# The order of the twelve matrix products of a weight load in the input projection of a hybrid block

## The chip, the cores and the metric

The kernel runs on one core of one Trainium2 chip. The metric is the device time of one execution in microseconds (us): the median of three runs for the kernel before. One further execution was profiled; its span and its trace are what is read here. Engines are named as in the profile: PE is TensorE's matmul, PEld its weight load, DVE is VectorE, ACT is ScalarE, POOL is GpSimd, SP is SyncE, which issues most DMAs.

## What is computed

One layer of a backbone block on 256 latent tokens, with 256 context tokens in front of them, all in float32 and width 2048. Both token sets are normalised and modulated, and multiplied with the input projection `w_in`; its columns feed four groups of mixers: gated linear attention (GLA), gated DeltaNet (GDN), a short convolution, and RWKV-7. The recurrent ones scan forwards and backwards; they run on the context first, and their final states start the latent scans. Then come the output projection `w_out`, a gated residual, a SwiGLU feed-forward part and a final norm.

```python
def _mix(n, row_len, init, lp):
    (g_q, ..., r_wa, r_g) = jnp.split((n @ lp['w_in']).astype(jnp.float32), offs, axis=-1)
    ...                                   # GLA, GDN, short convolution, RWKV-7 on these columns
    y = jnp.concatenate([y_gla, y_gdn, y_sc, y_rw], axis=-1)
    return y @ lp['w_out'], states

o_c, ctx_states = _mix(modnorm(ctx), len_ctx, zero, lp)
o_x, _ = _mix(modnorm(x), GRID_W, ctx_states, lp)
h_x = h_x + m_x[2] * o_x
h_x = h_x + m_x[5] * swiglu(modnorm(h_x), w_gu, w_down)
return rmsnorm(h_x, final_g)
```

## The kernel before

**Precision.** A float32 product is made of three faster ones. Each operand is split in an upper part, rounded to the matmul's short format (`wh`, `H`), and the rest (`wl`, `L`): `wh H + wh L + wl H`. ACT makes `wh` from the raw weights (L197), then DVE subtracts to get `wl` (L202). Matmuls of the recurrent mixers are not split; PE runs each of them as two pieces (a transpose as one), and the profile counts pieces.

**The projection.** `proj` makes one tile of 128 output columns by 256 tokens in PSUM (`big`, two buffers). It goes over the 16 slices of the width in four loads (`hf`). A load takes 512 columns of weights by DMA into `wraw` (a ring of six), splits them into `wh` and `wl` (rings of three), and then makes 4 slices x 3 = 12 products; the accumulation starts with the first product of the tile and ends with the last. There are 66 tiles, so 264 loads and 3168 products. Between load and products up to two pieces of other work are taken from `feed`: matmuls `ob`, which make the later modulation vectors during the context stage.

**The mixers.** Two streams of recurrent work run side by side: stream a (RWKV-7; tiles `ea`, `la`, `iva...`, `rw_...`) and stream b (GDN and GLA; `eb`, `lb`, `ivb...`, `gd_...`). Each is a chain of small matmuls with steps on ACT, DVE or POOL between them. A GLA pair does for each direction: scores (`eb<-gd_q,gd_Fb`), transposes (`eb<-ident,gd_Fg`), and four scan steps of matmuls into `lb`, with the state `gd_S` between them; after both directions a sum for the norm (`lb<-gd_tok,ones`), and then the result goes as `yH`, `yL` to the output projection.

**What sets the order.** The table `ORDER` lists the parts (RWKV, GDN, GLA, projections to be parked in DRAM, short convolutions), with an offset of priority for some. Tile's scheduler then orders each engine's instructions when the program is built: of what is ready in its own account of time, it issues what has the highest priority. Loads and splits of weights stand in `high_priority`, so they run as early as their rings allow; products have their part's priority. Each engine works through its order strictly, and waits where an input is missing. The output projection (`wout`, L1486 on) uses the same rings; for the first two column blocks it goes over the tiles 12 to 15, 4 to 11 and then 0 to 3, which GLA makes; each load gives six products on 512 columns.

Of the kernel before, what the change touches and what calls it, by code (L numbers as in the profile page):

```python
# [18 lines left out]
KT = D // P  # L19
# [156 lines left out]
def block_kernel(ctx: ExitStack, tc: tile.TileContext, x, cx, ada_first, ada_later, ada_b, w_in, w_early, w_out,  # L176
# [11 lines left out]
    def mk(pool, shape, tag, bufs=None, dt=F32):  # L188
        pool = sub.get(tag[:3], pool) if pool is sub.get("mx") else pool
        return pool.tile(list(shape), dt, tag=tag, name=nm(tag), bufs=bufs)  # L190
# [22 lines left out]
    def mm(o, l, r, start=True, stop=True):  # L213
        return TE.matmul(o, l, r, start=start, stop=stop)  # L214
# [35 lines left out]
    def wraw():  # L250
        return mk(wp[0], [P, wp[1]], "wraw", wp[3])

    def split(raw, who, pool=None):

        n = 2 if pool else wp[2]
        h = mk(pool or wp[0], [P, wp[1]], "wh", n, F32R)
        l = mk(pool or wp[0], [P, wp[1]], "wl", n, F32R)

        n = 2 if wp[1] == 1024 else 1
        w = wp[1] // n  # L260
        for i in range(n):
            sl = slice(i * w, (i + 1) * w)
            acopy(h[:, sl], raw[:, sl])
            tt(l[:, sl], raw[:, sl], h.bitcast(F32)[:, sl], SUB, e=who)
        return h, l
# [120 lines left out]
    with ExitStack() as st:  # L386
# [76 lines left out]
        for kt in range(KT):  # L463
# [4 lines left out]
            with tc.issue_after(ins if kt != KT - 2 else after):  # L468
                for i in range(NE):
                    o = acc[i // 2][:, i % 2]  # L470
                    a, b = wh[:, i * P:(i + 1) * P], wl[:, i * P:(i + 1) * P]
# [40 lines left out]
    with mix:  # L512
# [36 lines left out]
        def PB(shape, tag="e"):  # L549

            tag = tag if tag == "big" else tag + cur[0]
            return mk(pb, shape, tag, 2 if tag in ("big", "ea") else 1)
# [43 lines left out]
        def proj(nHL, which):  # L596

            r0 = TIDX[which] * P
            H, L = nHL
            ps = PB([P, T], "big")  # L600
            for hf in range(4):
                with tc.high_priority():
                    raw = wraw()
                    nc.sync.dma_start(raw, w_in[r0:r0 + P, hf * 512:(hf + 1) * 512])
                    wh, wl = split(raw, V)
                for f in feed[:2]:
                    f()
                del feed[:2]
                for k in range(4):
                    kt = hf * 4 + k  # L610
                    a, b = wh[:, k * P:(k + 1) * P], wl[:, k * P:(k + 1) * P]
                    mm(ps, a, H[kt], kt == 0, False)
                    mm(ps, a, L[kt], False, False)
                    mm(ps, b, H[kt], False, kt == KT - 1)
            return ps

        def pcol(nHL, name, i):
            return proj(nHL, (name, i))
# [813 lines left out]
        for tok in ORDER:  # L1432
            st, _, ofs = tok.partition(":")
            with tc.high_priority(offset=int(ofs)) if ofs else ExitStack():
# [4 lines left out]
                elif low == "pd":  # L1439
                    park([(n, c) for n in (dkv, dkv + ("d_q", "d_z"))[s] if s or (n, c) not in EARLY], s)  # L1440
                elif low == "pg":
                    park(gnames[c] + (gmore[c] if s else []), s)
                elif low == "xx":
                    if c == 0:
                        nHL = load_nT()
                        smx = t1("rgate")
                        acopy(smx, proj(nHL, ("small", 0)))
                    else:
                        sms[1] = smalls(smx)
                        prg = pcol(nHL, "r_g", 0)  # L1450
                        rg, tmp = t1("rgate"), t1("gd_k")
                        logsig(rg, prg, tmp)
                        act(rg, rg, AF.Exp)
                elif low == "ff":
                    for f in feed:
                        f()
                    del feed[:]
                elif low == "sc":
                    short_conv(c, nHL)
                elif low == "yy":  # L1460
                    finish("a")
                    rws.close()
                    yp = mix.enter_context(tc.tile_pool(name="yp", bufs=1, reuse_waits="tile"))
                    yH, yL = ([mk(yp, [P, T], f"y{n}{i}", 1, F32R) for i in range(16)] for n in "HL")
                    yt += [yH, yL]
                else:
                    dict(gd=gd, rw=rw, gl=gl)[low](c, s)
# [56 lines left out]
        for k2 in range(KT // 2):  # L1524
            pt = PB([P, 2, T], ("big", "l", "big", "e", "e")[k2 % 5])
            for kk in range(2):
                kt = 2 * k2 + kk
# [3 lines left out]
            for kk in range(2):  # L1531
                kt = 2 * k2 + kk
                b = modB[:, 2, kt:kt + 1]
                n, h, l = nn[:, kk], N2[kt][:, 0], N2[kt][:, 1]
# [28 lines left out]
    for f in range(FT):  # L1563
# [6 lines left out]
        for k0, nk, bufs in ((0, 8, wide), (8, 4, narrow), (12, 4, narrow)) if f == 0 else ((0, 8, wide), (8, 8, wide)):  # L1570
# [10 lines left out]
            for k, u in sorted(ku) if f == 0 else ku:  # L1581
                kt = k0 + k
                a, b = (t[:, k * P:(k + 1) * P] for t in w[u])
# [17 lines left out]
    for q in range(4):  # L1601
        ps = mk(ps2, [P, 512], "acc", 8)
# [6 lines left out]
    for b in range(4):  # L1609
# [3 lines left out]
        for k2 in range(FT // 2):  # L1613
# [9 lines left out]
            for j, (k2, wh, wl) in [(j, w) for j in range(2) for w in kept] if len(kept) == 4 else \  # L1623
                    [(j, (k2, wh, wl)) for j in range(2)] if not tail else ():
                for k in range(2):
                    kt, cs = 2 * k2 + k, slice(k * 512, (k + 1) * 512)
# [7 lines left out]
    for j in range(2):  # L1634
        r = mk(p5, [P, 1], "r", 3)
# [40 lines left out]
```

## Time and profile before

| | |
|---|---|
| median of three runs | 2000.33 us (1997.1 to 2002.27) |
| profiled execution | 1993.64 us, its span 1991.9 us |
| granted clock over the span | 0.99 |
| PE busy | 1896.2 us (95%) |
| weight loads busy | 1624.0 us (82%) |
| DVE busy | 1356.5 us (68%) |
| ACT busy | 1023.8 us (51%) |

How to read it: an engine's busy time is the union of its instructions; matmuls overlap (a product is recorded with 0.28 us where the next starts 0.12 us later), so PE's work is better read from starts. The span has these stages: first modulation vectors, normalisation of the context and the first projections until about 155 us; context mixers with most of the `ob` matmuls until about 400 us, with the load of the latent tokens at the end; latent mixers and projections until about 1109 us; the last projections and the output projection until 1222.7 us; then the feed-forward part.

### The profile page before, as it was taken

Reading aid. Unit: us, or ns where it says so; the run is one execution under the profiler, and the core shown is the slowest. Engines: PE = TensorE matmul, PEld = TensorE weight load, DVE = VectorE, ACT = ScalarE, POOL = GpSimd, SP = SyncE. Lnnn points to the kernel's source line nnn. Section 1 sums busy time; section 2 is a strip of 40 time slices with the busy share of each in tenths; the row PEclk is TensorE's granted clock in tenths of the full one; section 3 lists DMA queues with packets and bytes.
Section 4 is the critical chain, followed back from the end, with each engine's and each line's share of the span. In section 5 each row is a group of like instructions: output and inputs, shape, how many; then the busy total and the mean of one; then the engine's idle time right before and its main releaser. Section 6 shows DMA issues by size and latency. Waiting matters only on the chain.

```text
span 1991.9 us, 36160 instructions
## 1 busy us (share of the span) xinstructions
PE 1896.2 (95%) x13312; PEld 1624.0 (82%) x13312; DVE 1356.5 (68%) x3327; ACT 1023.8 (51%) x2125; POOL 160.0 (8%) x207
## 2 busy tenths in 40 slices
PE   5998999999999999999999998999999999999997
PEld 3776777787878888888998977888888888888886
DVE  4446856898877789899767566996555555555554
ACT  2225645566565555566455555455555555544443
POOL 0002000000001000101001001111001010000000
PEclk9999999999999999999999999999999999999999
DMA  8976685444367432222244665896555555565554
GB/s 347 403 302 214 218 264 186 128 129 153 98 207 230 146 106 67 91 77 74 93 160 146 211 189 183 291 323 229 187 189 183 189 186 185 202 210 192 194 196 149
DMA packets 162081, 374.66 MB, mean 188 GB/s; under 512 B 17896, under 2 KB 43752, under 8 KB 156784
## 3 DMA queue, kind: packets, MB, share of 16 engines
q1 hardware_dynamic: 156288, 368.21, 53.9%
q10 hardware_dynamic: 5616, 4.14, 0.7%
q8 instruction: 104, 1.70, 0.4%
q14 instruction: 73, 0.60, 0.1%
HBM read 360.48 MB, written 11.80 MB: 187 GB/s over the span
## 4 chain that ended last, share of the span: by engine, by line
PE 79%; DVE 10%; ACT 5%; DMA 4%; issue 2%; POOL 0%; SPq 0%; ACTq 0%; DVEq 0%; POOLq 0%
PE acc L214 40%; PE big L214 15%; PE la L214 6%; PE ea L214 5%; PE lb L214 4%; DVE wl L202 3%; PE eb L214 3%; PE ob L214 3%; ACT wh L197 2%; DMA wraw<-in_w_in 1%; DMA wraw<-in_ada_later 1%; PE pt L214 0%; ACT rw_z L193 0%; DVE ivaXc L202 0%; DVE ivaw L202 0%
## 5 line engine op out<-in xcount | busy, mean ns | idle before, releaser
L202 DVE TENSOR_TENSOR wl<-wraw,wh 128x512 fp32r<-128x512 f32 x856 | 569.2, 691 | 390.5 <-ACT wh L197 382.4
L197 ACT ACTIVATE wh<-wraw 128x512 fp32r<-128x512 f32 x856 | 510.0, 626 | 508.3 <-PE acc L214 193.9
L214 PE MATMUL acc<-n,wh 128*128 128x512 f32 x1408 | 494.1, 400 | 3.1 <-ACT wh L197 3.1
L214 PE MATMUL acc<-n,wl 128*128 128x256 f32 x1408 | 382.6, 282 | 0.3 <-DVE wl L202 0.3
L214 PE MATMUL big<-nh,wh 128*128 128x256 f32 x1056 | 315.9, 300 | 3.7 <-ACT wh L197 2.9
L214 PE MATMUL big<-nh,wl 128*128 128x256 f32 x1056 | 310.9, 295 | 1.3 <-DVE wl L202 1.3
L214 PEld LDWEIGHTS acc<-n,wh 128*128 128x128 f32 x1408 | 260.4, 189 | 59.6 <-ACT wh L197 3.4
L214 PE MATMUL big<-nl,wh 128*128 128x256 f32 x1056 | 306.8, 291 | 0.0
L214 PEld LDWEIGHTS acc<-n,wl 128*128 128x128 f32 x1408 | 268.2, 190 | 9.8 <-DVE wl L202 1.2
L214 PEld LDWEIGHTS big<-nh,wh 128*128 128x128 f32 x1056 | 199.7, 189 | 22.2 <-issue 12.5
L214 PEld LDWEIGHTS big<-nh,wl 128*128 128x128 f32 x1056 | 199.7, 189 | 7.8 <-issue 3.1
L214 PEld LDWEIGHTS big<-nl,wh 128*128 128x128 f32 x1056 | 199.8, 189 | 3.5 <-issue 2.9
L214 PE MATMUL acc<-wl,hH 128*128 128x512 f32 x352 | 137.2, 390 | 0.3 <-DVE wl L202 0.2
L214 PE MATMUL acc<-wh,hH 128*128 128x512 f32 x352 | 137.4, 390 | 0.0
L214 PE MATMUL acc<-wh,hL 128*128 128x512 f32 x352 | 137.0, 389 | 0.0
L214 PE MATMUL ob<-wraw,sc 128*32 128x128 f32 x1536 | 85.9, 286 | 10.8 <-DMA wraw<-in_ada_later 7.2
L202 POOL TENSOR_TENSOR hL<-sg,hH 128x256 fp32r<-128x256 f32 x44 | 47.4, 1078 | 451.3 <-ACT hH L197 451.3
L214 PEld LDWEIGHTS acc<-wl,hH 128*128 128x128 f32 x352 | 66.1, 188 | 15.1 <-DVE wl L202 1.4
L214 PEld LDWEIGHTS acc<-wh,hH 128*128 128x128 f32 x352 | 66.1, 188 | 13.9 <-ACT up L197 0.2
L214 PEld LDWEIGHTS acc<-wh,hL 128*128 128x128 f32 x352 | 66.1, 188 | 13.8
L214 PEld LDWEIGHTS ob<-wraw,sc 128*32 128x32 f32 x1536 | 39.0, 110 | 37.3 <-DMA wraw<-in_ada_later 11.2
L202 DVE TENSOR_TENSOR wl<-wr,wh 128x1408 fp32r<-128x1408 f32 x16 | 26.0, 1623 | 42.9 <-ACT wh L197 42.9
(483 smaller groups left out, 3169.3 us busy)
## 6 DMA issues: line engine op xcount, KB each, us to landing
wraw<-in_w_gu SPq DMA_DIRECT2D x174, 512.0 KB, 3.4
wraw<-in_w_in SPq DMA_DIRECT2D x264, 256.0 KB, 3.0
wraw<-in_ada_later SPq DMA_DIRECT2D x256, 256.0 KB, 4.0
wraw<-in_w_down SPq DMA_DIRECT2D x88, 512.0 KB, 4.2
ad<-in_ada_first SPq DMA_DIRECT2D x32, 1024.0 KB, 10.3
wraw<-in_w_out SPq DMA_DIRECT2D x64, 256.0 KB, 2.8
wr<-in_w_early SPq DMA_DIRECT2D x16, 704.0 KB, 6.2
xin<-in_cx SPq DMA_DIRECT2D x2, 1024.0 KB
```

The costliest lines, as they stand in the source:

```text
L197: A.activation(o, i, AF.Copy)
L202: (e or V).tensor_tensor(out=o, in0=a, in1=b, op=op)
L214: return TE.matmul(o, l, r, start=start, stop=stop)
```

## The change

The lower part's product comes first of the three, the twelve products are put in a list, and all but the first of them are traced in `high_priority`. What was the start and stop of an accumulation stays at the first and the last product of a tile.

```diff
                 del feed[:2]
+
+                todo = []
                 for k in range(4):
                     kt = hf * 4 + k
                     a, b = wh[:, k * P:(k + 1) * P], wl[:, k * P:(k + 1) * P]
-                    mm(ps, a, H[kt], kt == 0, False)
-                    mm(ps, a, L[kt], False, False)
-                    mm(ps, b, H[kt], False, kt == KT - 1)
+                    todo += [(b, H[kt]), (a, H[kt]), (a, L[kt])]
+                for i, (l, r) in enumerate(todo):
+                    with tc.high_priority() if i else ExitStack():
+                        mm(ps, l, r, hf == i == 0, hf == 3 and i == len(todo) - 1)
             return ps
```

In the rows of an order, `out<-in` names the tiles with a number each, and the columns follow. Before, on PE, a load of an early context projection: `wh_2056` and `wl_2057` are its parts, `nh`, `nl` the tokens' parts, `eb` and `ea` recurrent groups.

```order
L214 MATMUL big_2023<-nh_24_106,wh_2056 128x256
L214 MATMUL big_2023<-nl_40_122,wh_2056 128x256
L802 MATMUL eb_1484<-ident_64,smd_227_1436 128x128
L214 MATMUL ea_1542<-smd_227_1436,sw_90 128x256
L802 MATMUL eb_1484<-ident_64,smd_228_1438 128x128
L214 MATMUL ea_1545<-smd_227_1436,sw_90 128x256
L214 MATMUL big_2023<-nh_24_106,wl_2057 128x256
L214 MATMUL ea_1558<-rw_sq_1556,consts_89 128x256
L214 MATMUL big_2023<-nh_25_107,wh_2056 128x256
L214 MATMUL big_2023<-nl_41_123,wh_2056 128x256
```

Now, the same load on PE, from its first product on:

```order
L214 MATMUL big_2023<-nh_24_106,wl_2057 128x256
L214 MATMUL big_2023<-nh_24_106,wh_2056 128x256
L214 MATMUL big_2023<-nl_40_122,wh_2056 128x256
L214 MATMUL big_2023<-nh_25_107,wl_2057 128x256
L214 MATMUL big_2023<-nh_25_107,wh_2056 128x256
L214 MATMUL big_2023<-nl_41_123,wh_2056 128x256
L214 MATMUL big_2023<-nh_26_108,wl_2057 128x256
L214 MATMUL big_2023<-nh_26_108,wh_2056 128x256
L214 MATMUL big_2023<-nl_42_124,wh_2056 128x256
L214 MATMUL big_2023<-nh_27_109,wl_2057 128x256
L214 MATMUL big_2023<-nh_27_109,wh_2056 128x256
L214 MATMUL big_2023<-nl_43_125,wh_2056 128x256
```

The recurrent groups that stood inside the load come behind it, and the product with `wl` leads each three.

The second place is the forward direction of the last GLA pair on latent tokens. Before, on PE, projection products stand between its scores (`gd_Fb`) and its transposes (`gd_Fg`), and go on behind them:

```order
L214 MATMUL eb_13765<-gd_q_13758,gd_Fb_13732 128x64 x4
L214 MATMUL big_13977<-nl_751_3843,wh_13998 128x256
L214 MATMUL big_13977<-nh_750_3842,wl_13999 128x256
L214 MATMUL big_13977<-nh_754_3852,wh_13998 128x256
L214 MATMUL big_13977<-nl_755_3853,wh_13998 128x256
L214 MATMUL big_13977<-nh_754_3852,wl_13999 128x256
L214 MATMUL big_13977<-nh_758_3862,wh_13998 128x256
L214 MATMUL big_13977<-nl_759_3863,wh_13998 128x256
L214 MATMUL big_13977<-nh_758_3862,wl_13999 128x256
L214 MATMUL big_13977<-nh_762_3872,wh_14016 128x256
L214 MATMUL big_13977<-nl_763_3873,wh_14016 128x256
L1336 MATMUL eb_13772<-ident_64,gd_Fg_13734 128x128 x4
```

Now, on PE, the same direction; `ea_14629` is the output projection's second column block, and `yL_2716` the first GLA pair's result:

```order
L214 MATMUL ea_14629<-wl_14989,yH_2700_11898 128x512
L214 MATMUL ea_14629<-wh_14988,yL_2716_11914 128x512
L214 MATMUL eb_13765<-gd_q_13758,gd_Fb_13732 128x64 x4
L1339 MATMUL eb_13772<-ident_64,gd_Fg_13734 128x128 x4
L214 MATMUL lb_13781<-gd_vt_13742,gd_dl_13777 128x128
L214 MATMUL lb_13781<-gd_Fg_13734,gd_vt_13742 128x128
L214 MATMUL lb_13781<-gd_Fb_13732,gd_S_3149_13779 128x128
L214 MATMUL eb_13806<-smd_1548_7015,sw_90 128x256
L214 MATMUL lb_13788<-gd_vt_13742,gd_dl_13777 128x128
L214 MATMUL lb_13788<-gd_Fg_13734,gd_vt_13742 128x128
L214 MATMUL lb_13788<-gd_Fb_13732,gd_S_3151_13785 128x128
L214 MATMUL lb_13795<-gd_vt_13742,gd_dl_13777 128x128
```

The pair's steps now follow each other without products between them, and what stands ahead is the output projection. The backward direction goes on in the same way, down to these rows on PE, where the pair's norm (`lb_13870`) is followed by the output products of the tile that it makes (`yH_2701`):

```order
L214 MATMUL lb_13857<-gd_Fb_13732,gd_S_3170_13854 128x128
L214 MATMUL lb_13864<-gd_Fg_13734,gd_vt_13742 128x128
L214 MATMUL lb_13864<-gd_Fb_13732,gd_S_3172_13861 128x128
L214 MATMUL lb_13870<-gd_tok_13868,ones_65 128x512
L214 MATMUL big_14626<-wh_14944,yH_2701_11899 128x512
L214 MATMUL big_14626<-wl_14945,yH_2701_11899 128x512
```

Before, the same norm stands among the output products: 79 of them are ahead of it, and those of other tiles come next.

## Rows read from the trace of the kernel before

**Rows 1.** The page's first section: busy us, share of the span, instructions.
```profile
PE 1896.2 (95%) x13312; PEld 1624.0 (82%) x13312; DVE 1356.5 (68%) x3327; ACT 1023.8 (51%) x2125; POOL 160.0 (8%) x207
```

**Rows 2.** Busy time by stage; the first line names the columns.
```profile
core 0: us, PE busy (x) PEld busy (x) DVE busy (x) ACT busy (x) POOL busy (x), PEclk, DMA share, GB/s
...
155.00:400.00 245.00, 225.52 (x2135) 180.54 (x2133) 171.65 (x543) 136.80 (x313) 22.93 (x41) 0.97 0.64 206
400.00:1003.00 603.00, 581.80 (x4748) 517.60 (x4748) 513.36 (x1605) 351.79 (x779) 55.38 (x84) 1.00 0.38 125
1003.00:1109.00 106.00, 102.24 (x794) 96.38 (x793) 72.70 (x157) 57.30 (x126) 10.87 (x9) 1.00 0.43 144
```

**Rows 3.** The page's costliest groups: busy us, mean ns, idle before, releaser.
```profile
L214 PE MATMUL big<-nh,wh 128*128 128x256 f32 x1056 | 315.9, 300 | 3.7 <-ACT wh L197 2.9
L214 PE MATMUL big<-nh,wl 128*128 128x256 f32 x1056 | 310.9, 295 | 1.3 <-DVE wl L202 1.3
```

**Rows 4.** Busy time of two dense stretches: projection products, then output products.
```profile
1110.00:1126.00 16.00, 16.00 (x138) 16.00 (x137) 9.96 (x20) 10.09 (x20) 0.00 (x0) 1.00 0.51 168
...
1150.00:1200.00 50.00, 50.00 (x214) 39.98 (x213) 31.03 (x50) 26.53 (x47) 0.00 (x0) 1.00 0.65 185
```

**Rows 5.** Timeline of PE: start us, duration us, instruction, tiles, shape, count.
```profile
646.04 0.28 PE L214 MATMUL big<-nh,wh 128*128 128x256 f32 x1
646.23 1.16 PE L214 MATMUL la<-ivaW,ivaL 128*128 128x128 f32 x8
647.14 0.37 PE L214 MATMUL big<-nl,wh 128*128 128x256 f32 x1
647.35 0.28 PE L214 MATMUL big<-nh,wl 128*128 128x256 f32 x1
...
1003.08 1.16 PE L214 MATMUL eb<-ivbW,ivbX 128*128 128x128 f32 x8
...
1099.80 0.28 PE L214 MATMUL big<-nh,wl 128*128 128x256 f32 x1
1099.92 0.39 PE L214 MATMUL lb<-gd_vt,gd_dl 128*128 128x128 f32 x2
1100.14 0.39 PE L214 MATMUL lb<-gd_Fg,gd_vt 128*128 128x128 f32 x2
1100.36 0.39 PE L214 MATMUL lb<-gd_Fb,gd_S 128*128 128x128 f32 x2
1100.50 0.36 PE L214 MATMUL big<-nh,wl 128*128 128x256 f32 x1
1100.70 0.63 PE L214 MATMUL big<-nh,wh 128*128 128x256 f32 x2
```

**Rows 6.** Timeline of PE, the recurrent steps of the two latent GLA pairs.
```profile
1057.09 0.39 PE L214 MATMUL lb<-gd_Fb,gd_S 128*128 128x128 f32 x2
...
1058.53 1.12 PE L214 MATMUL lb<-gd_tok,ones 128*128 128x512 f32 x2
...
1076.96 1.08 PE L214 MATMUL eb<-gd_q,gd_Fb 128*128 128x64 f32 x8 [0.59 <-DVE gd_Fb L202]
...
1086.64 0.39 PE L214 MATMUL lb<-gd_Fb,gd_S 128*128 128x128 f32 x2
...
1088.49 1.10 PE L214 MATMUL eb<-gd_q,gd_Fb 128*128 128x64 f32 x8 [1.00 <-DVE gd_q L211]
```

**Rows 7.** Timeline of ACT, the first pair's result for the output projection.
```profile
1063.68 0.40 ACT L197 ACTIVATE yH<-y_o 128x256 fp32r<-128x256 f32 x1
```

**Rows 8.** Instructions of the tile `wl` from 1003 to 1104 us.
```profile
L202 DVE TENSOR_TENSOR wl<-wraw,wh x43: 666/691/1533, 1003.6 to 1103.2; 128x512 fp32r<-128x512 f32 x43
```

**Rows 9.** Busy time of a stretch at the lower granted clock, columns as above.
```profile
344.78:355.01 10.23, 9.14 (x60) 6.91 (x59) 6.47 (x17) 4.32 (x10) 1.39 (x2) 0.50 0.74 247
```

## The prediction

> **What bounds the kernel now.** I read the page's first section, then the busy time by stage, then the costliest groups, and at last the timeline of PE at the places that the order of the changed program points to. PE is busy for 95% of the span [rows 1], so the first question is where it is not. By stage [rows 2]: from 155 to 400 us (context tokens, and the load of the latent ones) it is busy for 225.5 of 245 us, so something else sets the pace there; from 400 to 1003 us for 581.8 of 603; from 1003 to 1109 us, where the last recurrent work runs, for 102.2 of 106. From 1109 to about 1223 us it never idles: what projections are left, then the output projection. So from 400 us on PE's own work is the time, and there are two ways to change it: make that work smaller, or leave PE without something to do. The recurrent work of the mixers hops from PE to ScalarE or VectorE and back; projection products are what PE does meanwhile.
>
> The edit's own subject is hardly a cost now. Of the 1056 products of each kind, those that read `wh` waited 2.9 us in all for ScalarE, and those that read `wl` 1.3 us for VectorE [rows 3].
>
> **The change part by part.**
> *The lower part first.* A load's twelve products can now start only when `wl` is there, while before the first two products needed only `wh`. A product in a dense stretch takes 16.00 / 138 = 0.116 us [rows 4], so two give 0.23 us of cover per load. If every one of the 264 loads came just in time, this would cost 264 x 0.23 = 61 us. Behind the waiting product stand, on PE, the other eleven and the next recurrent group, so such a wait is passed on to the chain. But the 1.3 us say that `wl` is mostly there long before the third product. Bounds 0 and 61; I take 1, by the waits. The weights' DMAs keep their number, queue and ring, and from 400 to 1003 us the DMA engines are busy for 0.38 of the time [rows 2]: no bound there.
>
> *Nothing between them.* In PE's order before, products stand in 399 runs of 1 to 192; in the new order there are 190, each a multiple of 12. Total instructions are the same. What a broken run costs is seen in two places [rows 5]. At 646.04 us a product, eight pieces of a recurrent group and a product take until the next product at 647.35: 1.31 us. Dense, two products (0.23) and eight pieces at 0.11 (two take 1100.14 - 1099.92 = 0.22) would be 1.11: the break costs 0.20. At 1099.80 a product, six pieces and a product take until 1100.70: 0.90, dense 0.23 + 0.66 = 0.89: the break costs 0.01. I take the middle, 0.1 us. Of the 209 breaks that go, 70 are in the context stage, where PE waits anyway, and I count them at nothing (if PE were the bound there they would give 7 us). 139 go after it: -13.9 us. In the output projection there is 1 break now that becomes 26 (below): +2.5. Net -11.4; bounds 0, and (209 - 25) x 0.20 = -37.
>
> In the dense stretch weight loads are busy for 16.00 of 16.00 us, from 400 to 1003 us for 517.6 of 603 [rows 2, 4]. The Trainium skill, Trace Analysis, "Identifying the Most-Contended Engine", holds matmul busy time a bad measure, since matmuls are pipelined, and goes by the weight loads' share. By that rule PE has 603 - 517.6 = 85 us of room there and not 603 - 581.8 = 21, and the breaks would be worth their dear end, -37 instead of -11.4. [...]
>
> *What moves.* A block of twelve is 1.4 us of PE, and once begun nothing passes it; a recurrent step that gets ready meanwhile waits. Counted in the new order, the latent RWKV work begins after 1764 products where it began after 1007, and stays late by 470 to 600 products. The products that it used to run beside are used up before it ends. Before, 192 products and then all of the output projection stand behind the last recurrent group that matters; now the last products are followed by output products with the rest of the recurrent work between them, and the last 40 recurrent instructions (both directions of the second GLA pair) have nothing between them at all. Output products of tiles 2 and 3 stand behind and wait for their result. The same holds for the last GDN head's norm, which tile 7 waits for directly.
>
> The price: the recurrent chain from there to the end took, before, from 1003.08 us [rows 5] to 1088.49, the start of the last backward direction [rows 6]: 85.4 us. That last direction then was slowed by filling; the forward one took from 1076.96 to 1086.64 + 0.39 = 10.1 us. From its end to the norm's sum, and to the tile that the output products read, the first pair took 1058.53 - 1057.48 (end of its last step) = 1.0 and 1063.68 + 0.40 - 1058.53 = 5.6 [rows 6, 7]. Sum 102 us. PE's own work in that piece of the new order is 160 output products at 50.00 / 214 = 0.234 us [rows 4] = 37.4, and the recurrent instructions: 80 of 128 and 16 of 64 columns at 0.22 (two pieces each), 24 transposes at 0.11 (one piece), and, by their columns, an estimate from those rows, 13 of 256 at 0.44 and 2 of 512 at 0.88: 31. Together 69, so 33 us are left idle. The chain will go somewhat faster: 43 splits of weights stood on VectorE in that time [rows 8], now there are 160 / 6 = 27. If the 16 that go (0.69 us each, 11 us) had all stood in its way, 22 are left; if half, 27. I take 27; bounds 22 and 33. That I read this from the order makes its place sure, not its size.
>
> *The clock.* From 344.78 us the granted clock was 0.50 (the lower of its two levels, 1.2 GHz) for 10.23 us, in the stage in which PE has gaps [rows 9]; half of that, 5 us, is what such a fall can cost. The bare piece at the end should bring one: +4, bounds 0 and 10.
>
> *Other idle time.* Between 400 and 1003 us PE idles 21 us now [rows 2]. With coarser filling each recurrent step has more work ahead of it, so PE should come to it later and wait less: -5; bounds -21, and +10 if the new order puts steps back to back that need each other (in its latent stage up to 24 recurrent instructions stand together).
>
> Sum: +1 - 11.4 + 27 + 4 - 5 = +15.6 us. Against the profiled execution (1993.64 us) that is 2009; its time lies 6.7 us under the median of the three runs (2000.33), the scale on which the new kernel is timed, so 2016 there. The gains of my list are the better bounded below, and the larger break price is as well seen as the small: I shade by 3, to 2013.
>
> **The rivals.** *Faster:* the breaks decide. At the dear price, 0.20, and with the context stage PE-bound too, -37, and idle time down by 10, against 22 + 4 + 1 at the end: -20, so 1980 us. For it: PE is the bound from 400 us on, and the group of eight, the dear one, is the usual size. Against: many breaks sat where PE waited a little anyway. It wins where a break costs over 0.18 us. (The rule of Trace Analysis above would end here.)
> *Nothing to be seen:* all 209 - 25 breaks count, at 0.15: -28, idle time -5, against 27 + 4 + 1 at the end: 1999 us.
> *Slower by far:* VectorE is the second bound (513.4 of 603 us busy [rows 2]) and `wl` stands in its queue behind recurrent steps; if PE loses half of the cover, 0.12 us, at every load, +31: 2044 us. Against it are the waits of 1.3 us.
> *It doesn't do what it says:* by the order it does; no chance of its own.
>
> **How the numbers follow.** About what a measurement here can tell from no change is 0.3%, 6 us. The forecast (slower, an exposed end that the saved breaks don't pay) gets 0.56, its own range 2005 to 2026; no difference 0.23; faster 0.14; far slower 0.07. The range from 1993 to 2033 leaves out most of the fast rival and of the slow one. Faster by over 6 us: 0.15; within: 0.24; slower: 0.61.
>
> **What would show it.** Right: PE's busy time falls by 10 to 20 us from fewer breaks, and a hole of 25 us or more stands just before the end of the output projection, with waits of PE for `gd_Fb`, `gd_dl` and the state `gd_S`, and a granted clock of 0.50 in or behind it; the output projection ends later than at 1223 us. Wrong: PE stays above 90% busy through the last GLA pair (the end is hidden after all), or PE's wait for `wl` grows to tens of us (the far slower rival), or the stage from 400 to 1000 us loses as much as the end does.

## The result and the profile after

The changed kernel takes 2046.91 us (median of four runs, 2043.16 to 2047.34), the kernel before 2001.3 us beside it: a ratio of 1.0225, 95% interval 1.0205 to 1.0245. So it is slower, as predicted, but by 46 us and not by 13, and outside the range. The profiled execution of it took 2043.16 us, 49.5 more than that of before.

The page's first section and two of its costliest groups, columns as in [rows 1, 3]:

```profile
PE 1906.7 (93%) x13312; PEld 1627.3 (80%) x13312; DVE 1357.8 (67%) x3327; ACT 1024.2 (50%) x2125; POOL 159.0 (8%) x207
...
L214 PE MATMUL big<-nh,wl 128*128 128x256 f32 x1056 | 319.5, 303 | 1.6 <-ACT xs L197 0.6
L214 PE MATMUL big<-nh,wh 128*128 128x256 f32 x1056 | 299.9, 284 | 0.0
```

The products with `wl`, which now lead, wait 1.6 us in all, and the page puts none of it down to `wl`. PE's busy time did not fall, it rose by 10.5 us. A matmul that doesn't stand in a dense row, or runs at the lower clock, is recorded longer (a product behind a recurrent group 0.37 us against 0.28 [rows 5]; an output product 0.63 at the lower clock, at the end of this document, against 0.40), so this number can't show saved work.

Busy time by stage, the first three as in [rows 2], the fourth from the last projection product to the last output product:

```profile
155.00:400.00 245.00, 222.16 (x2094) 174.92 (x2092) 162.93 (x512) 131.37 (x298) 20.17 (x40) 0.96 0.64 205
400.00:1003.00 603.00, 574.45 (x4795) 521.46 (x4794) 498.60 (x1509) 353.72 (x777) 53.17 (x78) 0.98 0.43 135
1003.00:1109.00 106.00, 96.13 (x738) 90.05 (x738) 73.25 (x206) 46.22 (x96) 4.80 (x7) 0.97 0.34 110
1109.00:1271.00 162.00, 140.62 (x640) 108.35 (x639) 94.22 (x191) 75.08 (x152) 9.95 (x9) 0.91 0.42 127
```

The loss sits in the last line. Before, the output projection stood dense behind the last projection product, from 1132.0 to 1222.4 us, 90.4 us; now the last projection product comes at 1109.8, 22 us earlier, but the last output product at 1270.91, after 161.1 us. PE's waits there, the largest:

```profile
engine line waited for: us in total, times, longest us
PE big L214 <- ACT yH L197: 6.9, 3, 3.3
PE eb L1339 <- DVE gd_Fg L202: 2.5, 2, 1.5
PE lb L214 <- DVE gd_qe L202: 1.9, 3, 0.6
PE lb L214 <- ACT gd_qe L197: 1.5, 2, 0.7
PE lb L214 <- ACT gd_dl L197: 1.4, 2, 0.7
```

These are steps of the last GDN head and the two GLA pairs, and the results that output products read. The timeline of PE around the last GLA norm, and the last output product:

```profile
1212.79 2.07 PE L214 MATMUL lb<-gd_tok,ones 128*128 128x512 f32 x2 [1.04 <-ACT gd_tok L193]
1218.16 0.79 PE L214 MATMUL big<-wh,yH 128*128 128x512 f32 x1 [3.29 <-ACT yH L197]
1218.75 0.63 PE L214 MATMUL big<-wl,yH 128*128 128x512 f32 x1
...
1270.91 0.40 PE L214 MATMUL ea<-wh,yL 128*128 128x512 f32 x1
```

The norm starts at 1212.79; before it started at 1150.64. From it to the last output product pass 58.1 us, before 71.8.

**Where the 22 us went.** A length says little where work has moved, so I set each stretch of PE against its dense work: products at 0.116 us and output products at 0.234 [rows 4], a recurrent piece at 0.11 for 128 columns. What is left is idle or slow time, "loss" below. In the output projection stood 89.7 us of output products and, before, almost nothing else; now there are 246 recurrent pieces too, 29.5 us. So 161.1 - 89.7 - 29.5 = 41.9 us are loss (before -0.2). PE idles for 162.00 - 140.62 = 21.4 us of it; in the rest it is busy, but slower than in a dense row. And of the 22 us by which projections end earlier nothing was gained: 28.6 us of work had moved behind them.

### The profile page after: what moved, and what is told of

It reads as the page before. It is cut to its first block, busy times and chain, and to the rows that moved or that the text cites. A ratio compares the mean times of both kernels' runs of the same rounds, so it can differ in the third digit from the quotient of the medians.

```text
span 2041.3 us, 36110 instructions
## 1 busy us (share of the span) xinstructions
PE 1906.7 (93%) x13312; PEld 1627.3 (80%) x13312; DVE 1357.8 (67%) x3327; ACT 1024.2 (50%) x2125; POOL 159.0 (8%) x207
## 4 chain that ended last, share of the span: by engine, by line
PE 67%; DVE 15%; DMA 8%; ACT 6%; issue 3%; POOL 1%; SPq 0%; ACTq 0%; DVEq 0%; POOLq 0%
PE acc L214 36%; PE big L214 12%; PE la L214 5%; DVE wl L202 4%; PE ea L214 4%; PE lb L214 3%; DMA wraw<-in_w_in 3%; DMA wraw<-in_ada_later 3%; PE eb L214 2%; ACT wh L197 2%; PE ob L214 2%; DVE ivaXc L202 1%; DVE ivaw L202 1%; ACT rw_z L193 0%; PE pt L214 0%
## 5 line engine op out<-in xcount | busy, mean ns | idle before, releaser
L214 PE MATMUL big<-nh,wl 128*128 128x256 f32 x1056 | 319.5, 303 | 1.6 <-ACT xs L197 0.6
L214 PE MATMUL big<-nh,wh 128*128 128x256 f32 x1056 | 299.9, 284 | 0.0
L214 PE MATMUL big<-nl,wh 128*128 128x256 f32 x1056 | 299.5, 284 | 0.0
L214 PEld LDWEIGHTS big<-nh,wl 128*128 128x128 f32 x1056 | 202.3, 192 | 20.1 <-issue 13.7
L214 PEld LDWEIGHTS ob<-wraw,sc 128*32 128x32 f32 x1536 | 41.1, 110 | 46.5 <-DMA wraw<-in_ada_later 15.5
L214 PEld LDWEIGHTS acc<-wh,hL 128*128 128x128 f32 x352 | 66.1, 188 | 13.6
```

## The experiments

Loss by stretch, in us, of the profiled execution of every kernel: context (first projection product to the first transpose of the latent tokens), load (to the last such transpose), latent (to the last projection product), end (to the last output product). The last columns: time at the granted clock of 0.50 from 150 us to the last projection product, and from the last GLA norm to the last output product. The table's losses at the end lie up to 0.3 us above the count by hand (42.1 for 41.9); in g1 the matmuls that nobody reads count as loss.

| kernel | median | ratio to before, 95% | context | load | latent | end | at 0.50 | norm to end |
|---|---|---|---|---|---|---|---|---|
| before | 2001.3 | | 36.8 | 14.4 | 97.6 | 0.1 | 17.0 | 71.8 |
| changed | 2046.91 | 1.0225 [1.0205, 1.0245] | 39.7 | 21.7 | 92.6 | 42.1 | 44.3 | 58.1 |
| e1 lower part first only | 1992.36 | 0.9947 [0.9931, 0.9964] | 37.4 | 14.8 | 93.3 | 0.1 | 17.0 | 114.2 |
| e2 blocks only | 2020.59 | 1.0098 [1.0062, 1.0133] | 32.6 | 19.2 | 83.3 | 34.1 | 20.4 | 57.9 |
| e3 blocks in the context | 1998.6 | 0.998 [0.9964, 0.9995] | 35.6 | 16.9 | 98.7 | -0.1 | 23.8 | 114.2 |
| e4 blocks in the latent part | 2027.22 | 1.011 [1.0085, 1.0134] | 37.0 | 20.5 | 83.9 | 34.5 | 23.8 | 58.0 |
| f1 no blocks, late start | 2043.07 | 1.022 [1.0193, 1.0247] | 35.4 | 13.6 | 109.0 | 32.4 | 27.2 | 57.4 |
| f2 blocks of six | 2018.0 | 1.0099 [1.008, 1.0119] | 31.4 | 21.8 | 97.4 | 21.6 | 20.4 | 58.3 |
| f3 blocks of three | 2009.3 | 1.0058 [1.0037, 1.0078] | 40.2 | 17.7 | 93.5 | 11.0 | 17.0 | 57.1 |
| f4 changed, early start | 2030.59 | 1.0162 [1.0141, 1.0182] | 36.6 | 21.8 | 88.1 | 33.4 | 30.6 | 57.7 |
| g1 changed, holes filled | 2037.77 | 1.0205 [1.0181, 1.0229] | 43.7 | 19.9 | 95.9 | 34.7 | 54.5 | 55.1 |
| g2 blocks late | 2009.99 | 1.0065 [1.0046, 1.0083] | 35.1 | 13.3 | 84.1 | 30.3 | 17.0 | 57.6 |
| g3 blocks early | 2006.3 | 1.0034 [1.0021, 1.0048] | 43.2 | 21.7 | 90.8 | 6.6 | 47.7 | 57.2 |
| g4 blocks first | 2017.33 | 1.0104 [1.0087, 1.0121] | 43.9 | 21.5 | 104.7 | 0.1 | 51.2 | 114.2 |

(The kernel before ran beside each group of kernels on their chip: 2003.1 us beside e1 to e4, 1998.6 beside the f's, 1998.26 beside the g's; the ratios are to these. A block: products of one load that stand together on PE, twelve where nothing else is said. Theory E: the exposed end, that is, the recurrent chain's last steps with too little other work left to run beside them. W: the wait for `wl`. B: blocks hold up ready steps wherever they are. The expectations count norm to end from the norm's second piece, 1 us less.)

**e1, e2: each half of the change alone.** e1 is the change with

```diff
-                    with tc.high_priority() if i else ExitStack():
+                    with tc.high_priority() if False else ExitStack():
```

> The lower part's product leads each three, but no product stands in high priority. In PE's order the products again stand in 397 runs (399 before, 190 in the changed kernel), and 131 recurrent instructions stand behind the last projection product (133 before, 242 in the changed kernel). Theory E (exposed end: the blocks push the recurrent chain back, and its rest runs bare beside the output projection): as before, 2001 us, within 6; last projection product at about 1132 us, last output product at about 1222 us. Theory W (the wait for the lower part is the cost, as in the far slower rival): about 2030 to 2046 us, with idle time of PE in front of the products that read wl.

e2 keeps the high priority and the old order of the three:

```diff
-                    todo += [(b, H[kt]), (a, H[kt]), (a, L[kt])]
+                    todo += [(a, H[kt]), (a, L[kt]), (b, H[kt])]
```

> The products in the old order of the three (both products with wh first), but the last eleven of a load in high priority. 210 runs of products; 213 recurrent instructions behind the last projection product. Theory E: the 71 us that the changed kernel lost after its last projection product go with the 109 recurrent instructions that had moved behind it, so 80 of them cost 52 us; of the 22 us that it had gained until then (209 runs fewer) 189 runs fewer give 20. So about 2001 + 32 = 2033 us. Theory W: without the early wait for wl the blocks only gain: about 1981 us. Theory B (blocks hold up ready recurrent steps everywhere, and the end is only where it is seen): as the changed kernel, 2047 us, and with the last projection product later than at 1115 us.

e1 is even faster than before, by 0.5%, and nearly 3 us faster than E's range: the order of the three costs nothing, and W falls. e2 has the loss at the end (34.1 us). E's 52 us was too much and its 2033 us 12 too high; the last projection product at 1098 us contradicts B.

**e3, e4: the blocks in one part.** `if i and H is H0` and `if i and H is not H0`; `H0` are the context's tokens.

> The changed order of the three everywhere, but high priority only for the products of the context tokens. 327 runs; from the first latent recurrent work on the order is as with no priority, and 131 recurrent instructions stand behind the last product. Theory E: the end is as before; the 70 runs saved lie where PE waits anyway: 1994 to 2003 us, nearest 1999. Theory W: 2030 to 2046 us. Theory B: part of the loss, by the share of the context's loads (about a fifth): 2010 us.

> The changed order of the three everywhere, but high priority only for the products of the latent tokens. 263 runs; 212 recurrent instructions behind the last projection product. Theory E: 79 of 109 of the 71 us, that is 51, less 136 of 209 runs of the 22 us, that is 14: about 2038 us; last projection product near 1118 us, last output product near 1259 us. Theory W: 2030 to 2046 us, but with PE waiting in front of products that read wl. Theory B: four fifths of the loss spread over the latent stage, about 2037 us, with the last projection product near 1132 us or later.

The context's blocks do nothing to the end, the latent ones bring 34.5 of its 42.1 us: E holds there, and PE waited only 0.7 us for `wl` in e4 from 700 us to its last product. But E's 2038 us was 11 too high, and the halves don't add up in time: e3 is 0.2% faster than before and e4 1.1% slower, both together 2.25%.

**f1: the same end without blocks.** e1, and one number of the table:

```diff
-XX1 GD0:-100 RW0:50 PR1
+XX1 GD0:-100 RW0:-2400 PR1
```

> No blocks: the lower part leads each three, no product in high priority, and the first latent RWKV part gets an offset of -2400 in the table instead of 50, so that its recurrent work starts late. 398 runs of products (before 399), but 216 recurrent instructions stand behind the last product, as many as with blocks for the latent tokens (212). Theory E (what costs is the recurrent chain that ends bare beside the output projection, whoever pushed it back): against the kernel without blocks (1992 us) idle and slow time of some 35 us in the output projection as in the two runs with blocks (34.1 and 34.5), nothing gained before: 2020 to 2032 us. Theory B (the blocks themselves cost, by holding up ready steps at every place; a late chain alone finds enough to fill with): 1992 to 2003 us.

2043 us, as slow as the changed kernel, with 398 runs of products as before. So a recurrent chain that starts late is enough. Blocks are one way to make it late. E's number was 11 us too low: the recurrent work also crowded together ahead of the end (latent loss 109.0). Its last norm and last output product:

```profile
1207.45 2.07 PE L214 MATMUL lb<-gd_tok,ones 128*128 128x512 f32 x2 [1.04 <-ACT gd_tok L193]
...
1264.80 0.39 PE L214 MATMUL ea<-wh,yL 128*128 128x512 f32 x1
```

**f2, f3, f4: shorter blocks, and blocks with an early start.** `if i % 6`, `if i % 3`; f4 is the changed kernel with `RW0:400`.

> The lower part first; of each load's twelve products, two blocks of six instead of one of twelve. 280 runs (397 without blocks, 190 with twelve), 164 recurrent instructions behind the last product (131, 242). Theory E, by the end: 33 more instructions at 34 / 81 us each give 14; 117 fewer runs at 0.07 us give -8: 1992 + 6 = 1998 us. Theory S (saved breaks are worth 0.1 us or more and the end is short enough to be hidden): 1980 us. Theory B (by the size of the block): half of the changed kernel's 47 us: 2015 us.

> The lower part first; blocks of three. 349 runs, 156 recurrent instructions behind the last product. Theory E: 25 instructions at 0.42 us give 10; 48 fewer runs at 0.07 give -3: 1999 us. Theory S: 1987 us. Theory B: a quarter of 47 us: 2004 us.

> The changed kernel, but the first latent RWKV part has an offset of 400 in the table instead of 50: the blocks stay (205 runs, 190 in the changed kernel), and the recurrent chain comes earlier (its latent work begins after 1272 products, 1764 in the changed kernel); 197 recurrent instructions stand behind the last product (242). Theory E: 66 more than without blocks at 0.42 us give 28, and the saved breaks (0.07 us for the latent ones) -8: 2003 to 2020 us, some 30 to 40 us faster than the changed kernel. Theory B: 2040 to 2047 us, as the blocks are as many and as long.

E's numbers were low by 10 to 20 us, B's lay nearer for f2 and f3, too high for f4. Counting instructions behind the last product is a poor measure: 74 recurrent pieces stand there in f2 with 21.6 us of loss, and 106 in g3 with 6.6. A better one is in the last column. Wherever the end is exposed, 57.1 to 58.3 us pass from the last norm to the last output product (55.1 in g1, see there): the norm's way to the output projection, 5.4 us in the changed kernel, and 216 output products, 50.5 us (235 in g3). In e1, e3 and g4 they are 114 us and the end is dense. The timelines of f3 and of e1, norm and last output product:

```profile
1180.96 1.12 PE L214 MATMUL lb<-gd_tok,ones 128*128 128x512 f32 x2 [1.45 <-ACT gd_tok L193]
...
1238.04 0.39 PE L214 MATMUL ea<-wh,yL 128*128 128x512 f32 x1
```

```profile
1105.53 1.02 PE L214 MATMUL lb<-gd_tok,ones 128*128 128x512 f32 x2
...
1219.75 0.39 PE L214 MATMUL ea<-wh,yL 128*128 128x512 f32 x1
```

So the kernel ends with the later of two things, PE's work and the recurrent chain plus 58 us. Before had 71.8 - 58 = 14 us to spare. The change moved the norm by 62.1 us; 62.1 - 14 = 48 is the delay of the last output product (48.5). By the same sum e2 (+34.6) gives 21 (measured 20.7), f1 (+56.8) 43 (42.4), f3 (+30.3) 16 (15.6). These sums are no test of their own: they say again that the distance is nearly the same in all of them.

**g1: is it the clock?** The changed kernel with 200 matmuls that nobody reads, of the lowest priority, so that they fill the holes of the output projection:

```diff
+        with tc.high_priority(offset=-100000):
+            junk = [mk(pb, [P, T], "ob", 1)]
+            for _ in range(200):
+                mm(junk[0], yH[13][:, :P], yH[13])
```

> The changed kernel and 200 more matmuls of 256 columns that nobody reads (one short-convolution result with itself, 0.116 us each, 23 us in all), of the lowest priority, so that they stand in the holes of the output projection: 195 of them between the last projection product and the last recurrent step. They shorten no wait. Theory C (a good part of the 42 us lost at the end is the half clock that follows the holes: 34.1 us of 0.50 between the last projection product and the feed-forward part, 6.8 before the change): the granted clock stays at 1.00 there and the time falls by 7 to 13 us, to 2034 to 2040. Theory L (latency of the recurrent chain alone; what PE does in the holes is indifferent): 2047 us, up to 2052 where a junk matmul stands in front of a step that is ready.

The stretch from the last projection product to the norm's second piece, of the changed kernel, and of this one (columns as in [rows 2]):

```profile
1110.00:1213.80 103.80, 85.71 (x414) 64.75 (x413) 59.65 (x134) 45.52 (x97) 9.95 (x9) 0.90 0.36 111
```

```profile
1114.50:1213.30 98.80, 96.39 (x581) 80.36 (x580) 59.35 (x134) 45.37 (x96) 9.99 (x9) 1.00 0.38 117
```

The granted clock is 1.00 and the stretch 5.0 us shorter, with the matmuls that nobody reads in it. From there to the last output product it is 2.6 us shorter too. Norm, first output product of the last pair, and last output product of g1:

```profile
1212.80 1.13 PE L214 MATMUL lb<-gd_tok,ones 128*128 128x512 f32 x2
...
1217.59 0.50 PE L214 MATMUL big<-wh,yH 128*128 128x512 f32 x1
...
1267.86 0.39 PE L214 MATMUL ea<-wh,yL 128*128 128x512 f32 x1
```

From the last projection product (1114.39) to the last output product pass 153.5 us, in the changed kernel 161.1. So in these two executions the clock at the end costs about 7.6 us, the low end of C's 7 to 13, and some 34 of the 42 us are the chain's latency. By the median the kernel gained 9 us, and L's 2047 lies outside its four runs; but the intervals of the two ratios overlap, so of the whole time the gain is not shown.

**g2, g3, g4: where the chain falls behind.** Blocks from the part `YY0` of the table on, up to it, and up to `XX1`:

```diff
+            if st == "YY0":
+                blocks.append(1)
...
-                    with tc.high_priority() if i else ExitStack():
+                    with tc.high_priority() if i and blocks else ExitStack():
```

(g3 and g4 start with `blocks` filled and clear it there.)

> The lower part first; blocks of twelve only for the parts traced behind the RWKV heads (the GLA and short-convolution projections, 24 of the 66 tiles). 364 runs (397 without blocks), and the RWKV work stands where it stands without blocks; 176 recurrent instructions behind the last product (131 without). In all six kernels with an exposed end so far the last output product comes 56 to 57 us after the last GLA norm (lb<-gd_tok,ones), and without blocks the norm has 113 us left. Theory E: blocks at the very end are enough to expose it, since the last GDN and GLA heads have no later place to catch up: 2010 to 2020 us, with the norm 57 us ahead of the last output product. Rival H (the delay is brought in at the head of the latent stage, where the first RWKV head starts 123 us late): 1990 to 2000 us.

> The complement: the lower part first, blocks of twelve only for the parts traced ahead of that place (42 of the 66 tiles). 244 runs; the latent RWKV work begins after 1764 products as in the changed kernel (without blocks 1242); 176 recurrent instructions behind the last product. Theory E: the chain is late from the head of the stage and catches up in part, since the last 24 tiles let it through: the norm 57 us ahead of the last output product, 2005 to 2020 us. Rival H: nearly all of the loss of the changed kernel, 2035 to 2047 us. Saved breaks: 153 fewer at 0.07 us are 11 us, seen as an earlier last projection product.

> The lower part first; blocks of twelve only for the context's parts and the first latent ones, up to the second part of the load of latent tokens. 294 runs (103 fewer than without blocks), 131 recurrent instructions behind the last product, as without blocks. Theory E: nothing is exposed; the saved breaks lie in the context and the first latent stage, where PE waits in part: 1990 us, within 5 (the kernel without blocks 1992). If a saved break were worth the 0.1 us of the prediction at every place: 1982 us. If the half clock in the load of the latent tokens (20.5 us of 0.50 in the changed kernel, 3.4 before) comes with the blocks there: 1996 to 2000 us.

g2 and g3 came as E said, and H falls: either half of the blocks exposes the end, neither accounts for the whole. (The 11 us by which g3's last projection product should come earlier were 3.0.) g4 missed all three numbers. Its end is dense, and yet it lost 24.6 us against e1: 6.5 in the context, 6.7 in the load, 11.4 in the latent stage. It stood 51.2 us at the lower clock ahead of the end, e1 17.0; half the difference is 17 us. The load stretch of e1 and of g4 shows it in the column after POOL, 0.96 and 0.82:

```profile
363.70:407.60 43.90, 37.49 (x285) 29.47 (x284) 39.17 (x125) 27.92 (x65) 2.14 (x3) 0.96 0.33 94
```

```profile
368.00:414.50 46.50, 37.40 (x257) 30.76 (x254) 39.73 (x122) 26.48 (x64) 2.87 (x5) 0.82 0.31 93
```

So a part of what blocks cost has nothing to do with the end. Of the 103 runs of products that g4 saves 35 lie in the latent stretch, the rest in the context and the load.

**How a block makes the chain late.** It is not only the 1.4 us of one block. In the changed kernel, of one group of eight pieces, `la<-rw_F,rw_kt`, six stand at 619.3 to 619.8 us and the last two at 649.2. (Before, the same group has six at 534.0 to 534.5 and the last two at 535.9.) The groups of PE instructions between, with the idle time before them last:

```profile
L214 PE MATMUL big<-nh,wl 128*128 128x256 f32 x76 | 21.9, 288 | 0.1
L214 PE MATMUL big<-nl,wh 128*128 128x256 f32 x76 | 21.4, 281 | 0.0
L214 PE MATMUL big<-nh,wh 128*128 128x256 f32 x76 | 21.4, 281 | 0.0
L214 PE MATMUL eb<-smd,ident 128*128 128x256 f32 x4 | 1.0, 379 | 0.0
L214 PE MATMUL eb<-ivbR,consts 128*128 128x480 f32 x2 | 1.0, 566 | 0.0
L214 PE MATMUL la<-rw_F,rw_kt 128*128 128x64 f32 x5 | 0.7, 276 | 0.0
```

228 products, nineteen blocks, stand between pieces that read the same tiles, and PE did not idle before the last two. The engine is full there; the time is lost 500 us later. The first latent front of stream a (`ea<-ivaR`) comes at 710.4 us, before at 587.5, and the last RWKV output 106 us late. That a late stream a makes the end of stream b late is seen where the offset of its first latent part is the only edit: in f1 the last GLA norm comes 101.9 us later than in e1, in f4 15.5 us earlier than in the changed kernel.

## Why the prediction failed

**The lower part first (+1).** Right: in the changed kernel PE waited 0.2 us for `wl` from 150 us to the last projection product, and e1 alone is not slower.

**Nothing between them (-11.4).** The price of 0.1 us was the middle of two places, but it held. A recurrent group starts late behind a product, by 0.084 us (median of 236 places of the trace of before, 415 to 1100 us), and the first product behind a group starts 0.079 us early (231). The early start is taken back one step later: the next product comes 0.086 us late (190 places), as in [rows 5], where 1100.50 to 1100.70 and 647.14 to 647.35 are 0.20 and 0.21 us instead of 0.116. Over the latent stretch, waits of over 0.5 us left out, the three kinds of steps sum to +25.6 - 16.0 + 26.0 = 35.6 us before and +5.0 - 4.9 + 15.5 = 15.6 in the changed kernel, with 139 fewer passages from products to recurrent work: 20.0 us saved, and 13.9 forecast for them. e1 and g1 show the same, 34.7 and 16.2.

**Other idle (-5).** This step failed. PE's idle time from 400 to 1003 us went from 21.2 to 28.6 us (603 less the busy time, [rows 2] and the stage rows above). In the changed kernel groups stand behind groups: in the latent stretch 23 steps from one group to another wait over 0.5 us, 22.8 us together, before 6 with 5.1. All waits of over 0.5 us sum to 36.2 us there, before 24.3; the most is for `rw_BK` from VectorE (9.2 us, before 3.6). The prediction had this as its upper bound, +10, for steps put back to back that need each other; it took more than half of what the breaks gave.

From the table: loss ahead of the end 154.0 now, 148.8 before; less half of the time at 0.50 (22.2 and 8.5) that is 131.8 and 140.3: -8.5 us in place of -15.4 for the three steps so far, part of which is the loss that went to the end with the moved groups.

**An exposed end (+27).** The place and PE's work were right: in front of the result of the last pair, at 1218.16, stand 168 output products (39.3) and 29.5 us of recurrent work, 68.8 us, and 69 were counted from the order. The size was off. The chain takes 108.4 us from the last projection product; in g1, where the clock stays at 1.00, it takes 103.2 (1114.39 to 1217.59). So the 102 of the sum was nearly right, and what failed is what was taken off it: of the 11 us for fewer splits on VectorE nothing came back. Without the cost of the clock the end loses 34 to 35 us (g1), which is the bare 102 - 69 = 33, and not 27.

**The clock (+4).** At the end about 7.6 us (g1), inside the bounds of 0 and 10. The larger failure is that I looked for it only there. Ahead of the end the changed kernel stood 44.3 us at 0.50, before 17.0: up to 13.7 us more, an estimate that takes half of the time at 0.50 as lost. It agrees with g1, which has the changed kernel's order up to there: 10.2 us more at 0.50, 5.5 us more loss. The longest piece stands in the load of the latent tokens:

```profile
397.60:414.70 17.10, 13.27 (x53) 11.25 (x53) 13.07 (x43) 6.65 (x17) 1.53 (x3) 0.50 0.11 32
```

Five kernels with the lower part first and blocks of twelve from the context into the first latent parts show 31 to 55 us at 0.50 ahead of the last projection product, the others 17 to 27. g4 and e1 differ in the blocks alone and have no time at 0.50 at the end, and over their whole spans g4 had a granted clock of 0.980 to 0.984 in four runs, e1 of 0.985 to 0.989 in six. So it is likely that the blocks bring it. But e2 has blocks in the same parts and only 20.4 us, and by which waits they would do it no run tells: the sums of waits differ by a few us only. That cause stays open.

**The sum.** End and its clock 42.0 (forecast 31), clock ahead of it 13.7 (forecast nothing, without a reason), the rest -8.5 (forecast -15.4): 47.2 (forecast 15.6), against 48.5 measured at the last output product. The sign and the main mechanism were right; three sizes failed, all toward more time: the exposed end, the clock, and the other idle time.

**The rivals.** The far slower one had the number, 2044, by a mechanism that did not occur: a coincidence. The faster one fell: the breaks gave 20 us and not 37, and the idle time rose. So did the rule of the Trainium skill, Perfetto Trace Analysis, "Identifying the Most-Contended Engine", as I had used it: PE's matmul time from 400 to 1003 us went down by 7.4 us and the weight loads' up by 3.9, and neither says what happened, since the time was set by a chain that no engine's busy share shows.

**The signs.** The late output projection, the hole and the lower clock came; of the three waits named, `gd_dl` (1.4 us, longer waits were for `gd_Fg` and `gd_qe`) and `gd_Fb` (0.6) came, and none for the state `gd_S`. The fall of PE's busy time did not come. The stretch with the GLA pairs stands at 83% (85.71 of 103.80 us, shown with g1).

## What to carry to other kernels

Where a scheduler fills the gaps of a long dependent chain with independent work, find how much later the chain could end before it sets the time (here 14 us, read as the distance from its last step to the end, against that distance when nothing else is left), and price an edit by what it does to that. Raising the priority of the filler looks free on a full engine, and is paid when the filler has run out. Price a switch between two kinds of work over the whole passage and over all places: here one step of it, the early start of the next product, looks like a gain, and the step behind it takes it back. And what fewer switches give can go again in waits between the groups that then stand together.

The version to keep is e1: the lower part first, no high priority, 0.9947 of before. Why it gains is open: its order differs little, its chain ends 45 us earlier, and in the profiled execution only 2.3 us of gain are seen.

## What the runs showed of the hardware

Behind the holes at the end the granted clock was 0.50 (the lower of its two levels, 1.2 GHz) for 23.9 us in one piece, where the kernel before has 10.23 at most [rows 9]:

```profile
1199.80:1223.70 23.90, 15.93 (x47) 11.46 (x47) 8.54 (x23) 6.26 (x14) 0.34 (x1) 0.50 0.01 1
```

It stayed at 0.50 while dense output products were running again from 1218.16 on. A product of 512 columns then takes 0.43 us from start to start (0.234 at 1.00), as here in another such piece, at 1142 us:

```profile
1142.35 0.63 PE L214 MATMUL big<-wl,yH 128*128 128x512 f32 x1
1142.78 0.63 PE L214 MATMUL big<-wh,yL 128*128 128x512 f32 x1
1143.21 0.63 PE L214 MATMUL big<-wh,yH 128*128 128x512 f32 x1
```
